# Feed-forward products with both parts of the activation in one 512-column matmul, and conditioning sums over rows of 1024

## The chip, the cores and the metric

The kernel runs on one core of a Trainium2 chip. A core has several engines that work side by side, each on its own queue of instructions: TensorE (in the profile PE for its matmuls and PEld for its weight loads), VectorE (DVE), ScalarE (ACT), GpSimd (POOL, nearly unused here), and SyncE (SP), which here issues the transfers. Work passes between engines by semaphores. Operands lie in SBUF; TensorE adds its results up in PSUM, which has eight banks of 512 float32 per partition.

The metric is the device time of one execution, in microseconds (us).

## The reference

The model is a trunk of two layers over 256 tokens of 1024 channels, in float32. Each layer is a feed-forward, a mixer (pooling in layer 0, differential attention in layer 1) and a second feed-forward, each under a norm whose scale, shift and gate come from a conditioning vector `c`:

```python
c_act = jax.nn.silu(c)
for i in range(DEPTH):                                   # 2
    mod = (c_act @ mod_w[i] + mod_b[i])[:, None, :]      # 1024 -> 9 * 1024
    sh0, sc0, g0, sh1, sc1, g1, sh2, sc2, g2 = jnp.split(mod, N_MOD, axis=-1)
    h = modulate(rms_norm(x, norm_g[i, 0]), sh0, sc0)
    x = x + 0.5 * g0 * swiglu(h, ffn_w_gu[i, 0], ffn_w_down[i, 0])
    h = modulate(rms_norm(x, norm_g[i, 1]), sh1, sc1)
    y = pool_mixer(h, ...) if i == 0 else diff_attention(h, ...)
    x = x + g1 * y
    h = modulate(rms_norm(x, norm_g[i, 2]), sh2, sc2)
    x = x + 0.5 * g2 * swiglu(h, ffn_w_gu[i, 1], ffn_w_down[i, 1])
return rms_norm(x, final_g)

def swiglu(h, w_gu, w_down):                             # 1024 -> 2 * 2816 -> 1024
    g, u = jnp.split(h @ w_gu, 2, axis=-1)
    return (jax.nn.silu(g) * u) @ w_down
```

There are four feed-forwards, of 34.6 MB of weights each, and 18 conditioning vectors of 1024, each from 4.2 MB of `mod_w`.

## The kernel before

**Split operands.** The products run in the type float32r, which keeps fewer bits than float32. So each operand is split into two parts, hi and lo, with hi + lo the float32 value. A product of two split operands is three matmuls, added up in PSUM: hi with hi, hi with lo, lo with hi. `prod3` (L341) issues them; its first operand is the one that TensorE loads (128 x 128), its second the moving one. In the feed-forward the weights are loaded and the activation moves: `hi` with `hh` (L343), `hi` with `hl` (L344), `lo` with `hh` (L345), each with a weight load of its own and 256 moving columns, the tokens. I call these three a triple.

**Weights.** `split_unit` (L278) fetches a unit of up to 512 rows by 256 columns (512 KB) into one of six `raw` buffers through SP's queue; ACT copies it to `hi` (L286) and DVE subtracts to `lo` (L287), seven buffers each. `unit` (L337) keeps five units prefetched.

**A feed-forward** (`ffn`, L490) has an up half of 11 steps. Step j makes two column blocks of 256, a gate block `pg` and an up block `pu`, each 16 triples over two units (`mm_half`, `mm_rows`, L451 and L460). The two 128-row results of a block lie side by side in one PSUM bank. ACT takes the SiLU of `pg` into SBUF (L511), DVE multiplies `pu` with it (L518), and the result is split into `ah`, `al` (L520). The down half has four blocks `dp` of 44 triples each over six units (`DOWN_K`); then `residual` (L405) adds the gated result to x and prepares the split operand `xh`, `xl` of the next stage, and `squares` (L412) adds up the sums that its norm needs.

In all but the first feed-forward the first two steps do not wait for the norm: `mm_deferred` (L435) multiplies the scaled x with two more columns for the shift (258 columns, L443 to L445), and the norm is applied to the result. In the first, five half blocks are begun early (`first_half`, L849), while the conditioning is worked out.

**Conditioning.** The first two vectors are worked out on TensorE at the start (`gemv_half`, L201). The 16 others are spread as steps between the blocks of the feed-forwards (`Background`, L260): six beside the first, four, five and one beside the others. A step of `gemv_steps` (L227) fetches two rows of 512 of `mod_w` per partition, 512 KB in all, and DVE adds them, times `cact`, to a sum of 512 columns (L239 the first, L241 the others): per vector 8 steps and 16 DVE instructions. At the end a matmul with ones (L246), a copy `row` (L249) and transposes (L252) turn two vectors at a time.

**PSUM.** `psum` hands out four single banks (tag `mm`), `psum2` two (tag `hd`), `psmall` two (tag `st`). The attention and the pooling mixer use the same functions.

**Order.** The program gives each instruction a priority by its place and by `high_priority`; a scheduler orders each engine's instructions at build time by these and by when buffers come free, so that PE's queue can interleave stages. On the chip every queue runs in that fixed order.

Of the kernel before, what the change touches and what calls it, by code (L numbers as in the profile page):

```python
# [33 lines left out]
U_BUFS = 8  # L34
# [3 lines left out]
def shape_constants():  # L38
    """Arrays that depend on the shapes alone: the pooling operator and the rotary tables."""
# [29 lines left out]
def trunk(ctx: ExitStack, tc: tile.TileContext, x, c, mod_w, mod_b, norm_g, w_gu, w_down, pool_w, pool_scale,  # L69
# [19 lines left out]

    def psum():  # L90
        return ps.tile([P, 512], F32, tag="mm", name=nm("mm"), bufs=4)

    def psum2():
        return ps.tile([P, 512], F32, tag="hd", name=nm("hd"), bufs=2)
# [21 lines left out]
    # ---------------------------------------------------------------- constants and small vectors  # L116
# [4 lines left out]
    # products on nothing, which bring the tensor engine to its full clock before the first data come  # L121
# [10 lines left out]
    hh = const([P, KD, T], "hh", F32R)  # L132
    hl = const([P, KD, T], "hl", F32R)
# [27 lines left out]
    # c and the rows of mod_w that it meets are dealt out eight in a row to a partition  # L161
# [8 lines left out]
    # ---------------------------------------------------------------- conditioning vectors  # L170
# [10 lines left out]
    def mod_done(i, p, k0=0, k1=KD):  # L181
        """Columns k0 to k1 of a conditioning vector are there: what the stages take from them."""
# [18 lines left out]
    def gemv_half(i, p, hf):  # L201
        """Half of silu(c) @ mod_w[i] + mod_b[i], 512 columns, transposed; on the tensor engine."""
        pt = psmall()
        # (while little else is there to do, products on nothing keep the tensor engine's clock up)
# [11 lines left out]
        row = t1k(512, "u", U_BUFS)  # L216
# [10 lines left out]
    def gemv_steps(parts):  # L227
        """The same for one or two parts, the sums over k tiles on the vector engine; a generator of steps."""
        n = 2 * len(parts)
        acc_ = [t1k(512, "u", U_BUFS) for _ in range(n)]  # L230
        for h in range(n):
            i, p = parts[h // 2]
            a = acc_[h]
            for q in range(4):
                rv = gemv_load(i, p, h % 2, q)
                for k in range(2):
                    kk = q * 2 + k
                    if kk == 0:
                        V.tensor_scalar(a, rv[:, k, :], cact[:, 0:1], None, ALU.mult)  # L239
                    else:  # L240
                        V.scalar_tensor_tensor(a, rv[:, k, :], cact[:, kk:kk + 1], a, ALU.mult, ALU.add)  # L241
                if h < n - 1 or q < 3:
                    yield
        pt = psmall()
        for h in range(n):
            PE.matmul(pt[h * 32:(h + 1) * 32, :], ones[:, 0:32], acc_[h], start=True, stop=True,  # L246
                      skip_group_check=True, tile_position=(0, h * 32))
        row = t1k(512, "u", U_BUFS)
# [11 lines left out]
    class Background:  # L260
        """Conditioning vectors worked out between the units of another stage, spread evenly over them."""
# [79 lines left out]
    def prod3(o, lh, ll, rh, rl, start, stop, **kw):  # L341
        """o += l^T r with both split."""
# [12 lines left out]
    # ---------------------------------------------------------------- norms  # L355
# [8 lines left out]
    def rsqrt_small(y, v, tiny=tiny):  # L364
        """y = v ** -0.5 on the vector engine: a first value from the exponent, then Newton steps."""
# [26 lines left out]
    def rstd_cols():  # L392
        """rstd of token q * 128 + p on partition p, column q."""
# [27 lines left out]
    def shift_cols(b):  # L421
        """The shift as two more columns of the moving operand."""
# [3 lines left out]
    def normalise(js, rstd, a, b):  # L426
        """h = x * a * rstd + b, split."""
# [7 lines left out]
    def mm_deferred(os_):  # L435
        """The products of one column block of 256 with x * a (and the shift); os_: the results of its two tiles."""
# [10 lines left out]
    def pair3(pt, m, lh, ll, rh, rl, first, last):  # L447
        """prod3 into half m of a bank whose halves are summed up side by side: the first product of half 0 clears it."""
        prod3(pt[:, m * T:(m + 1) * T], lh, ll, rh, rl, first and m == 0, last and m == 1, skip_group_check=True)

    def mm_half(pt, half, rh, rl, *ahead_):  # L451
        """Half of the products of one column block of 256 with 1024 rows of a split operand, transposed."""
# [10 lines left out]

    def shift_of(o):
# [4 lines left out]
    # ---------------------------------------------------------------- constants of the attention  # L469
# [19 lines left out]
    # ---------------------------------------------------------------- feed-forward  # L489
    def ffn(i, s, ndef, nxt, parts_up, parts_down, early=()):  # L490
        """nxt: scale of the next stage's norm, or None at the end."""
# [6 lines left out]
        for j in range(KF // 2):  # L498
# [4 lines left out]
            if j >= ndef:  # L503
                w = t1k(1024, "qk", 2)
                if early:
                    pg = early.pop(0)
                    mm_half(pg, 1, hh, hl)
                else:
                    pg = psum()
# [417 lines left out]
```

## Time and profile before

| | |
|---|---|
| median of 3 runs | 967.26 us (963.95 to 969.74) |
| span of the profiled execution, first to last instruction | 960.5 us |
| PE, PEld busy | 947.5, 911.9 us |
| DVE, ACT busy | 749.1, 498.6 us |
| HBM read | 234.34 MB, 245 GB/s over the span |
| transfers of `mod_w` | 144 of 512 KB, 5.7 us from issue to landing (median) |
| transfers of weights, up half | 176 of 512 KB, 5.2 us |

The page shows the profiled execution's span; the runs' times are a few microseconds longer, for what lies before the first and after the last instruction. Matmuls overlap in the array, so the duration of one (283 ns for 256 columns) is a latency; how often they start is what counts. A stretch of windows gives, for each engine, the busy time in it and the number of its instructions.

### The profile page before, as it was taken

What the parts mean: (1) busy time and instruction counts of PE and PEld (TensorE: products, weight loads), DVE (VectorE), ACT (ScalarE), POOL (GpSimd) and SP (SyncE); (2) the same over time, 40 slices, a digit from 0 to 9 for tenths busy, and PEclk for the clock granted to TensorE, in tenths of its full rate; (3) what the DMA queues carried; (4) which work ended last, traced back from release to release, by engine and by line L of the source; (5) the groups of instructions that cost most, each with busy time, mean ns of one, the idle gap of its engine ahead of it and who ended that gap; (6) DMA issues with size and microseconds to landing.
All of it is one profiled execution on the core that took longest, in us unless ns stands there. A gap on an engine that the chain in (4) does not pass through costs nothing.

```text
span 960.5 us, 19223 instructions
## 1 busy us (share of the span) xinstructions
PE 947.5 (99%) x7722; PEld 911.9 (95%) x7722; DVE 749.1 (78%) x1203; ACT 498.6 (52%) x759; POOL 0.7 (0%) x6
## 2 busy tenths in 40 slices
PE   8999999999999999999999999999999999999997
PEld 5699999999999999999999999989999999999996
DVE  3488889898998768888988788798888896664551
ACT  2354445455765445445654454367777764444541
POOL 0000000000000000000000000000000000000000
PEclk9999999999999999999999999999999999999999
DMA  8899999999469878997699888985544449765521
GB/s 280 285 337 319 325 319 321 317 346 292 140 192 344 268 242 277 312 313 255 195 344 315 289 280 300 297 286 168 153 135 128 140 154 292 234 222 180 181 78 44
DMA packets 201179, 237.69 MB, mean 247 GB/s; under 512 B 8113, under 2 KB 163074, under 8 KB 201090
## 3 DMA queue, kind: packets, MB, share of 16 engines
q1 hardware_dynamic: 200514, 235.42, 74.7%
q8 instruction: 60, 0.98, 0.4%
q10 hardware_dynamic: 576, 1.05, 0.3%
q14 instruction: 29, 0.24, 0.1%
HBM read 234.34 MB, written 1.05 MB: 245 GB/s over the span
## 4 chain that ended last, share of the span: by engine, by line
PE 91%; DVE 3%; DMA 3%; ACT 1%; issue 1%; SPq 0%; ACTq 0%; DVEq 0%
PE mm L343 22%; PE mm L344 21%; PE mm L345 21%; PE hd L344 4%; PE hd L345 4%; PE hd L343 4%; PE mm L445 2%; PE mm L443 2%; PE mm L444 2%; DMA raw<-in_mod_w_dram 1%; PE st L214 1%; PE st L246 1%; PE hd L655 1%; DVE lo L287 1%; DVE u L241 1%
## 5 line engine op out<-in xcount | busy, mean ns | idle before, releaser
L286 ACT ACTIVATE hi<-raw 128x1024 fp32r<-128x1024 f32 (+1 forms) x308 | 316.5, 1035 | 293.7 <-PE mm L344 146.1
L287 DVE TENSOR_TENSOR lo<-raw,hi 128x1024 fp32r<-128x1024 f32 (+1 forms) x308 | 363.5, 1192 | 57.7 <-ACT hi L286 54.5
L343 PE MATMUL mm<-hh,hi 128*128 128x256 f32 x992 | 280.2, 283 | 0.0
L345 PE MATMUL mm<-hh,lo 128*128 128x256 f32 x992 | 279.8, 283 | 0.0
L344 PE MATMUL mm<-hl,hi 128*128 128x256 f32 x992 | 279.7, 283 | 0.0
L343 PE MATMUL mm<-ahl,hi 128*128 128x256 f32 x768 | 217.4, 283 | 0.0
L344 PE MATMUL mm<-ahl,hi 128*128 128x256 f32 x768 | 216.6, 282 | 0.0
L345 PE MATMUL mm<-ahl,lo 128*128 128x256 f32 x768 | 216.1, 282 | 0.0
L241 DVE SCALAR_TENSOR_TENSOR u<-raw,cact,u 128x512 f32<-128x512 f32 x224 | 167.4, 749 | 55.4 <-DMA raw<-in_mod_w_dram 51.6
L343 PEld LDWEIGHTS mm<-hh,hi 128*128 128x128 f32 x992 | 186.8, 189 | 4.9 <-issue 3.4
L345 PEld LDWEIGHTS mm<-hh,lo 128*128 128x128 f32 x992 | 187.0, 189 | 1.1 <-issue 0.8
L344 PEld LDWEIGHTS mm<-hl,hi 128*128 128x128 f32 x992 | 186.9, 189 | 0.1
L343 PEld LDWEIGHTS mm<-ahl,hi 128*128 128x128 f32 x768 | 144.5, 188 | 6.2 <-issue 5.0
L344 PEld LDWEIGHTS mm<-ahl,hi 128*128 128x128 f32 x768 | 144.7, 188 | 0.9 <-issue 0.8
L345 PEld LDWEIGHTS mm<-ahl,lo 128*128 128x128 f32 x768 | 144.6, 188 | 0.0
L344 PE MATMUL hd<-hl,hi 128*128 128x256 f32 x288 | 81.4, 283 | 0.1
L343 PE MATMUL hd<-hh,hi 128*128 128x256 f32 x288 | 81.4, 283 | 0.0
L345 PE MATMUL hd<-hh,lo 128*128 128x256 f32 x288 | 81.2, 282 | 0.0
L444 PE MATMUL mm<-xl,hi 128*128 128x256 f32 x208 | 59.1, 286 | 0.0
L445 PE MATMUL mm<-xh,lo 128*128 128x258 f32 x208 | 58.6, 283 | 0.0
L443 PE MATMUL mm<-xh,hi 128*128 128x258 f32 x208 | 57.6, 283 | 0.1
L343 PEld LDWEIGHTS hd<-hh,hi 128*128 128x128 f32 x288 | 54.3, 189 | 1.8 <-ACT hh L432 0.9
(217 smaller groups left out, 1077.1 us busy)
## 6 DMA issues: line engine op xcount, KB each, us to landing
raw<-in_ffn_w_gu_dram SPq DMA_DIRECT2D x176, 512.0 KB, 5.2
raw<-in_mod_w_dram SPq DMA_DIRECT2D x144, 512.0 KB, 5.7
raw<-in_ffn_w_down_dram SPq DMA_DIRECT2D x64, 512.0 KB, 5.1
raw<-in_ffn_w_down_dram SPq DMA_DIRECT2D x32, 384.0 KB, 4.4
raw<-in_diff_w_qkv_dram SPq DMA_DIRECT2D x24, 512.0 KB, 4.8
raw<-in_diff_w_o_dram SPq DMA_DIRECT2D x8, 512.0 KB, 4.1
u<-in_x_dram ACTq DMA_DIRECT2D x4, 256.0 KB, 4.0
raw<-in_pool_w_dram SPq DMA_DIRECT2D x2, 512.0 KB, 6.1
```

Of the source, the lines that this page charges most:

```text
L214: PE.matmul(pt[r:r + 32, :], cwide[:, kk, :], rv[:, k, :], start=(kk < 4), stop=(kk >= 4), skip_group_check=True, tile_position=(0, r))
L241: V.scalar_tensor_tensor(a, rv[:, k, :], cact[:, kk:kk + 1], a, ALU.mult, ALU.add)
L246: PE.matmul(pt[h * 32:(h + 1) * 32, :], ones[:, 0:32], acc_[h], start=True, stop=True, skip_group_check=True, tile_position=(0, h * 32))
L286: S.activation(hi[:, :n], raw[:, :n], AF.Copy)
L287: V.tensor_tensor(lo[:, :n], raw[:, :n], hi[:, :n].bitcast(F32), ALU.subtract)
L343: PE.matmul(o, lh, rh, start=start, stop=False, **kw)
L344: PE.matmul(o, lh, rl, start=False, stop=False, **kw)
L345: PE.matmul(o, ll, rh, start=False, stop=stop, **kw)
L443: PE.matmul(o[:, :T + 2], hi[:, kk, cs], xh[:, k, :], start=(k == 0), stop=False)
L444: PE.matmul(o[:, :T], hi[:, kk, cs], xl[:, k, :], start=False, stop=False)
L445: PE.matmul(o[:, :T + 2], lo[:, kk, cs], xh[:, k, :], start=False, stop=(k == KD - 1))
L655: PE.matmul(sc[c2][:, q * T:(q + 1) * T], l[pr, 0, qs], r[pr, 1, :], start=(n == 0), stop=(n == 2))
```

## The change

**The wide product.** The two parts of the activation become one tile, `hhl`, with `hh` and `hl` as its halves (`ahl` was one already). `both` multiplies a hi tile with both at once, 512 moving columns, into a whole bank: hi with hh in the first half, hi with hl in the second. The lo tile meets `hh` alone, 256 columns, added to the second half. A block of two such banks is multiplied by `mm_wide` (up) or in the loop over `DOWN_K` (down). `fold` then copies the second halves to SBUF by ACT and adds the first ones by DVE; SiLU, product and residual read the result from SBUF. The early blocks, the deferred ones, the pooling mixer and the attention keep the triples.

**PSUM.** The banks are handed out in pairs: two of tag `mm`, one of tag `hd`. `wide` goes round over the three; `psum` and `psum2` hand out the halves of a pair one after the other.

**Conditioning.** A step fetches one row of 1024 columns per partition, again 512 KB, and adds it to a sum of 1024 columns: 8 DVE instructions per vector instead of 16. Four buffers of 1024 (tag `u`) take the place of eight of 512. Some users of that tag move to `qk`, among them `row`; others take a half of 1024.

Comments and docstrings are removed, so line numbers shift. The core of the diff:

```diff
-U_BUFS = 8
+U_BUFS = 4
...
+    def banks(tag, bufs):
+        return ps.tile([P, 2, 512], F32, tag=tag, name=nm(tag), bufs=bufs)
+    spare = {"mm": [], "hd": []}
+    def pair():
+        spare["mm"].clear()
+        return banks("mm", 2)
+    def pair2():
+        spare["hd"].clear()
+        return banks("hd", 1)
+    def one(tag, bufs):
+        if not spare[tag]:
+            t = banks(tag, bufs)
+            spare[tag] += [t[:, 0, :], t[:, 1, :]]
+        return spare[tag].pop(0)
     def psum():
-        return ps.tile([P, 512], F32, tag="mm", name=nm("mm"), bufs=4)
+        return one("mm", 2)
     def psum2():
-        return ps.tile([P, 512], F32, tag="hd", name=nm("hd"), bufs=2)
+        return one("hd", 1)
+    turn = [0]
+    def wide():
+        turn[0] += 1
+        return pair() if turn[0] % 3 else pair2()
...
-    hh = const([P, KD, T], "hh", F32R)
-    hl = const([P, KD, T], "hl", F32R)
+    hhl = const([P, 2, KD, T], "hhl", F32R)
+    hh, hl = hhl[:, 0], hhl[:, 1]
...
     def gemv_steps(parts):
         n = 2 * len(parts)
-        acc_ = [t1k(512, "u", U_BUFS) for _ in range(n)]
-        for h in range(n):
-            i, p = parts[h // 2]
-            a = acc_[h]
-            for q in range(4):
-                rv = gemv_load(i, p, h % 2, q)
-                for k in range(2):
-                    kk = q * 2 + k
-                    if kk == 0:
-                        V.tensor_scalar(a, rv[:, k, :], cact[:, 0:1], None, ALU.mult)
-                    else:
-                        V.scalar_tensor_tensor(a, rv[:, k, :], cact[:, kk:kk + 1], a, ALU.mult, ALU.add)
-                if h < n - 1 or q < 3:
+        acc_ = [t1k(1024, "u", U_BUFS) for _ in parts]
+        for e, (i, p) in enumerate(parts):
+            a = acc_[e]
+            for kk in range(KD):
+                raw = rawp.tile([P, 1024], F32, tag="raw", name=nm("raw"))
+                nc.sync.dma_start(raw, mod_w[i].rearrange("(p k) f -> p k f", p=P)[:, kk, p * D:(p + 1) * D])
+                if kk == 0:
+                    V.tensor_scalar(a, raw, cact[:, 0:1], None, ALU.mult)
+                else:
+                    V.scalar_tensor_tensor(a, raw, cact[:, kk:kk + 1], a, ALU.mult, ALU.add)
+                if e < len(parts) - 1 or kk < KD - 1:
                     yield
...
-        row = t1k(512, "u", U_BUFS)
+        row = t1k(512, "qk", 2)
...
+    def both(o, lh, ll, r, start, stop):
+        PE.matmul(o, lh, r, start=start, stop=False)
+        PE.matmul(o[:, T:], ll, r[:, 0, :], start=False, stop=stop)
+    def mm_wide(pt):
+        for half in range(2):
+            hi, lo = unit()
+            for m in range(2):
+                cs = slice(m * P, (m + 1) * P)
+                for kk in range(4):
+                    k = half * 4 + kk
+                    both(pt[:, m, :], hi[:, kk, cs], lo[:, kk, cs], hhl[:, :, k, :], k == 0, k == KD - 1)
+    def fold(out, pt):
+        S.activation(out, pt[..., T:], AF.Copy)
+        V.tensor_tensor(out, pt[..., :T], out, ALU.add)
...
                 else:
-                    pg = psum()
-                    mm_rows(pg, hh, hl)
-                S.activation(w[:, :512], pg, AF.Silu)
+                    pg = wide()
+                    mm_wide(pg)
+                    fold(w[:, :512].rearrange("p (m t) -> p m t", m=2), pg)
+                    S.activation(w[:, :512], w[:, :512], AF.Silu)
...
-                    pu = psum2() if j % 2 else psum()
-                    mm_rows(pu, hh, hl)
-                V.tensor_tensor(w[:, 512:], pu, w[:, :512], ALU.mult)
+                    pu = wide()
+                    mm_wide(pu)
+                    fold(w[:, 512:].rearrange("p (m t) -> p m t", m=2), pu)
+                    V.tensor_tensor(w[:, 512:], w[:, 512:], w[:, :512], ALU.mult)
...
-            po = psum()
+            po = wide()
...
-                            pair3(po, m, hi[:, k - k0, cs], lo[:, k - k0, cs], ah[:, k, :], al[:, k, :], k == 0, k == KF - 1)
+                            both(po[:, m, :], hi[:, k - k0, cs], lo[:, k - k0, cs], ahl[:, :, k, :], k == 0, k == KF - 1)
...
+                y = t1k(512, "qk", 2).rearrange("p (m t) -> p m t", m=2)
+                with tc.high_priority(offset=-100):
+                    fold(y[:, ms[0]:ms[-1] + 1, :], po[:, ms[0]:ms[-1] + 1, :])
                 if nxt or not last or ms[0] == 0:
-                    residual([js[m] for m in ms], [po[:, m * T:(m + 1) * T] for m in ms], g, a)
+                    residual([js[m] for m in ms], [y[:, m, :] for m in ms], g, a)
```

More of the change, by code (lines that the diff above doesn't have):

```diff
@@ L245, in gemv_steps @@
         for h in range(n):
-            PE.matmul(pt[h * 32:(h + 1) * 32, :], ones[:, 0:32], acc_[h], start=True, stop=True,
+            PE.matmul(pt[h * 32:(h + 1) * 32, :], ones[:, 0:32], acc_[h // 2][:, h % 2 * 512:(h % 2 + 1) * 512],
+                      start=True, stop=True,
                       skip_group_check=True, tile_position=(0, h * 32))
-        row = t1k(512, "u", U_BUFS)
+        row = t1k(512, "qk", 2)
         S.activation(row[:n * 32, :], pt[:n * 32, :], AF.Copy)
@@ L507, in ffn @@
                     mm_half(pg, 1, hh, hl)
+                    S.activation(w[:, :512], pg, AF.Silu)
                 else:
-                    pg = psum()
-                    mm_rows(pg, hh, hl)
-                S.activation(w[:, :512], pg, AF.Silu)
+                    pg = wide()
+                    mm_wide(pg)
+                    fold(w[:, :512].rearrange("p (m t) -> p m t", m=2), pg)
+                    S.activation(w[:, :512], w[:, :512], AF.Silu)
                 if early:
@@ L514, in ffn @@
                     mm_half(pu, 1, hh, hl)
+                    V.tensor_tensor(w[:, 512:], pu, w[:, :512], ALU.mult)
                 else:
-                    pu = psum2() if j % 2 else psum()
-                    mm_rows(pu, hh, hl)
-                V.tensor_tensor(w[:, 512:], pu, w[:, :512], ALU.mult)
+                    pu = wide()
+                    mm_wide(pu)
+                    fold(w[:, 512:].rearrange("p (m t) -> p m t", m=2), pu)
+                    V.tensor_tensor(w[:, 512:], w[:, 512:], w[:, :512], ALU.mult)
                 fs = slice(2 * j, 2 * j + 2)
@@ L522, in ffn @@
                 continue
-            pg = [psum(), psum()]
-            alloc = psum2 if j % 2 else psum
-            pu = [alloc(), alloc()]
+            pg, pu = wide(), wide()
+            pg, pu = ([t[:, m, :] for m in range(2)] for t in (pg, pu))
             sg = [t1k(), t1k()]
@@ L560, in ffn @@
                         for k in range(k0, k1):
-                            pair3(po, m, hi[:, k - k0, cs], lo[:, k - k0, cs], ah[:, k, :], al[:, k, :], k == 0, k == KF - 1)
+                            both(po[:, m, :], hi[:, k - k0, cs], lo[:, k - k0, cs], ahl[:, :, k, :], k == 0, k == KF - 1)
                     if ms[0] == 0:
                         back.tick()
+                y = t1k(512, "qk", 2).rearrange("p (m t) -> p m t", m=2)
+                with tc.high_priority(offset=-100):
+                    fold(y[:, ms[0]:ms[-1] + 1, :], po[:, ms[0]:ms[-1] + 1, :])
                 if nxt or not last or ms[0] == 0:
-                    residual([js[m] for m in ms], [po[:, m * T:(m + 1) * T] for m in ms], g, a)
+                    residual([js[m] for m in ms], [y[:, m, :] for m in ms], g, a)
                     squares([js[m] for m in ms])
                 else:
-                    residual([js[1]], [po[:, T:]], g)
+                    residual([js[1]], [y[:, 1, :]], g)
                     S.activation(sq7, xT[:, js[1], :], AF.Square)
@@ L601, in pool_mixer @@
             if g % 2:
-                cbt = t1k(512, *(("u", U_BUFS) if g < 2 else ("rope", 1)))
+                cbt = t1k(512, *(("qk", 2) if g < 2 else ("rope", 1)))
                 S.activation(cbt, pt, AF.Copy)
@@ L607, in pool_mixer @@
         for g in range(4):
-          z = t1k(512, "u", U_BUFS)
+          if g % 2 == 0:
+              zz = t1k(1024, "u", U_BUFS)
+          z = zz[:, g % 2 * 512:(g % 2 + 1) * 512]
           for q in range(NT):
@@ L660, in head_weights @@
             den = tinyw(4)
-            pe = [t1k(512, "u", U_BUFS) for _ in range(2)]
+            pe = t1k(1024, "u", U_BUFS)
+            pe = [pe[:, :512], pe[:, 512:]]
             for c2 in range(2):
@@ L818, in trunk @@
     for q in range(NT):
-        xq = [t1k(512, "u", U_BUFS) for _ in range(2)]
+        xq = t1k(1024, "u", U_BUFS)
+        xq = [xq[:, :512], xq[:, 512:]]
         for hf in range(2):
@@ L825, in trunk @@
         for hf in range(2):
-            S.activation(t1k(512, "u", U_BUFS), xin[q][hf], AF.Square, accum_out=ss[:, 2 * q + hf:2 * q + hf + 1])
+            S.activation(t1k(512, "qk", 2), xin[q][hf], AF.Square, accum_out=ss[:, 2 * q + hf:2 * q + hf + 1])
     v = tiny(NT)
@@ L897, in trunk @@
                 PE.transpose(pt[:, k * P:(k + 1) * P], xj[:, q * P:(q + 1) * P], ident)
-            ot = t1k(512, "u", U_BUFS)
+            if q == 0:
+                ott = t1k(1024, "u", U_BUFS)
+            ot = ott[:, q * 512:(q + 1) * 512]
             if q == 0:
```

## The prediction

> **What bounds the kernel now.** I began with the busy shares of the page.
>
> ```profile
> span 960.5 us, 19223 instructions
> ...
> PE 947.5 (99%) x7722; PEld 911.9 (95%) x7722; DVE 749.1 (78%) x1203; ACT 498.6 (52%) x759; POOL 0.7 (0%) x6
> ```
>
> TensorE and its weight loads are busy almost always, DVE four fifths. A busy PE need not be at its peak, so I read next, in the timeline, how far apart the products start.
>
> ```profile
> 300.00 0.28 PE L343 MATMUL mm<-hh,hi 128*128 128x256 f32 x1
> ...
> 302.97 0.28 PE L344 MATMUL mm<-hl,hi 128*128 128x256 f32 x1
> ...
> 800.04 0.29 PE L343 MATMUL hd<-hh,hi 128*128 128x256 f32 x1
> ...
> 803.04 0.28 PE L344 MATMUL hd<-hl,hi 128*128 128x256 f32 x1
> ...
> 258.56 0.28 PE L443 MATMUL mm<-xh,hi 128*128 128x258 f32 x1
> ...
> 261.68 0.28 PE L445 MATMUL mm<-xh,lo 128*128 128x258 f32 x1
> ...
> 15.06 0.59 PE L210 MATMUL mm<-raw,ident 128*128 128x256 f32 x2
> 15.28 0.59 PE L210 MATMUL mm<-raw,ident 128*128 128x256 f32 x2
> 15.49 0.38 PE L210 MATMUL mm<-raw,ident 128*128 128x256 f32 x1
> ```
>
> From 300.00 to 302.97 lie 25 starts: one product of 256 columns every 118.8 ns. From 800.04 to 803.04 another 25 come every 120.0 ns. From 258.56 to 261.68, where two in three have 258 columns, 26 come every 120.0 ns: the moving width does not separate these stretches. All three have one 128-column weight load per product. The products of L210 are plain fp32, which take longer over their 256 columns, and with the same weight load start every 215 ns (15.06, 15.28, 15.49): a load fits wholly behind a product that streams that long. I read 119 ns as the time of a weight load and its hand-over, with 256 columns streaming a little faster beneath it.
>
> Then the stages, by windows (columns: stretch, length, busy us of PE, PEld, DVE, ACT, POOL, granted clock, DMA share, GB/s).
>
> ```profile
> 53.00:172.00 119.00, 119.00 (x990) 116.07 (x989) 106.94 (x136) 57.09 (x68) 0.00 (x0) 1.00 0.98 325
> 175.00:237.00 62.00, 62.00 (x514) 60.05 (x513) 56.10 (x82) 31.67 (x43) 0.00 (x0) 1.00 1.00 327
> 258.00:282.00 24.00, 24.00 (x202) 23.91 (x201) 23.25 (x52) 17.08 (x27) 0.00 (x0) 1.00 0.69 215
> 282.00:377.00 95.00, 95.00 (x803) 94.27 (x801) 72.83 (x87) 43.48 (x52) 0.00 (x0) 1.00 0.82 270
> 379.00:442.00 63.00, 63.00 (x531) 61.98 (x530) 54.38 (x81) 29.35 (x39) 0.00 (x0) 1.00 0.94 316
> ...
> 472.00:570.00 98.00, 98.00 (x827) 97.03 (x826) 82.87 (x106) 47.53 (x56) 0.00 (x0) 1.00 0.91 301
> 573.00:637.00 64.00, 63.87 (x527) 61.73 (x526) 53.47 (x76) 28.66 (x38) 0.00 (x0) 1.00 0.91 303
> 642.00:748.00 106.00, 105.64 (x862) 101.03 (x862) 91.48 (x223) 78.42 (x193) 0.00 (x0) 1.00 0.48 146
> ...
> 788.00:878.00 90.00, 90.00 (x745) 88.82 (x744) 60.98 (x69) 41.99 (x49) 0.00 (x0) 1.00 0.74 237
> 878.00:943.00 65.00, 65.00 (x549) 65.00 (x549) 29.69 (x36) 27.72 (x37) 0.00 (x0) 1.00 0.36 118
> ```
>
> These are, in order, the up and down halves of the four feed-forwards, with the first deferred column blocks (258) and the attention (642) between. The clock is full. PE never idles, but the first feed-forward has DMA at 0.98 to 1.00 and DVE at 90%: there two others are nearly as late as PE.
>
> **The change, part by part.** *The wide product.* Three products with three loads (hi with hh, hi with hl, lo with hh) become two with two. How many:
>
> ```profile
> L343 PE MATMUL mm<-hh,hi 128*128 128x256 f32 x992 | 280.2, 283 | 0.0
> ...
> L343 PE MATMUL mm<-ahl,hi 128*128 128x256 f32 x768 | 217.4, 283 | 0.0
> ...
> L343 PE MATMUL hd<-hh,hi 128*128 128x256 f32 x288 | 81.4, 283 | 0.0
> ```
>
> Of 992 + 288 triples, 64 are the attention's q and k and 80 the five early blocks; of the 768, 64 are the attention's output product. That leaves 1136 + 704 = 1840 changed triples. A triple now costs 3 x 118.8 = 356 ns. After: the lo load hides behind the 512 columns, as a load does behind L210, so 215 ns for the wide product, then 119 for the narrow one, beneath which the next hi is loaded: 334 ns. The wide price is not in this trace. Its lower end is the 215 of L210 (under twice a 256-column stream it cannot go, and 256 columns stream in at most 119), its upper end two of today's products, 238. In between lies 119 + 107 = 226, if the 11 ns over L210's rate (215 / 2) belong to each instruction and not to its load. I take 215, the row whose stream and load lie nearest. Gross: 1840 x 22 ns = 40.5 us; by 226 it is 20 us, by 238 nothing.
>
> [...]
>
> *The fold.* Each changed block gets one ACT copy and one DVE addition out of PSUM. Prices:
>
> ```profile
> L287 DVE TENSOR_TENSOR lo<-raw,hi 128x1024 fp32r<-128x1024 f32 x276 | 333.5, 1220 | 46.7 <-ACT hi L286 43.5 <-DMA pk<-qk 1.6
> L241 DVE SCALAR_TENSOR_TENSOR u<-raw,cact,u 128x512 f32<-128x512 f32 x224 | 167.4, 749 | 55.4 <-DMA raw<-in_mod_w_dram 51.6
> ...
> L408 DVE SCALAR_TENSOR_TENSOR xT<-mm,G,xT 128x256 f32<-128x256 f32 x44 | 19.6, 478 | 19.0 <-PE mm L345 19.0
> ...
> L239 DVE TENSOR_SCALAR u<-raw,cact 128x512 f32<-128x512 f32 x32 | 15.4, 482 | 12.1 <-DMA raw<-in_mod_w_dram 12.1
> L518 DVE TENSOR_TENSOR qk<-mm,qk 128x512 f32<-128x512 f32 x21 | 14.4, 687 | 4.5 <-PE mm L345 4.3
> ...
> L249 ACT ACTIVATE u<-st 128x512 f32<-128x512 f32 x7 | 4.1, 589 | 5.8 <-PE st L246 5.8
> ```
>
> Up: 18 blocks in three feed-forwards, 17 in the first; down: 4 each: 87 folds. Addition like L518, 0.69 us; copy like L249, 0.59 us. DVE +60 us, ACT +51 us (52% to about 58%). The SiLU and the product stay, now from SBUF, at about the same price.
>
> *Conditioning in rows of 1024.* STT goes from 478 ns (256, L408) to 749 (512, L241): 271 per 256 elements, so 1024 cost about 1.29 us; the first, by L239 and the bounds 482 and 964, I take at 0.75. A vector goes from 2 x 0.482 + 14 x 0.749 = 11.45 us to 0.75 + 7 x 1.29 = 9.8: 1.7 saved, 16 vectors, 27 us of DVE. The DMAs stay 8 per vector of 512 KB, in the same places on SP's queue; rows are twice as long. [...]
>
> *Stage by stage* (PE after; DVE after = window + folds - 1.7 per vector; DMA as before):
> up 1: PE 119 - 17 x 16 x 0.022 = 113.0; DVE 106.9 + 11.7 - 6.8 = 111.8; DMA 0.98 x 119 = 116.6.
> down 1: PE 62 - 176 x 0.022 = 58.1; DVE 55.4; DMA 62.
> up 2: 88.7; 81.8; 78. down 2: 59.1; 53.7; 59.2.
> up 3: 91.7; 90.2; 89. down 3: 60.1; 52.8; 58.2.
> up 4: 83.7; 71.7; 67. down 4: 61.1; 32.4; 23.
> So the first feed-forward meets the DMA. What was prefetched (six raw, seven split buffers) covers part of it: I let it lose 4.9 of its 9.9 us, and the other near ties 1.5 together.
>
> *The ends of stages.* The next stage's products need the residual of the last block, which now waits for the fold, 0.59 + 0.69 = 1.28 us. Is there cover?
>
> ```profile
> 442.37 0.88 DVE L408 SCALAR_TENSOR_TENSOR xT<-mm,G,xT 128x256 f32<-128x256 f32 x2 [0.80 <-PE mm L345]
> ...
> 445.83 0.67 PE L383 MATMUL st<-acc,ones 128*128 128x256 f32 x2 [0.17 <-DVE acc L419]
> ```
>
> DVE waits for PE at once, and 3.5 us later PE already waits for the sum over squares: no cover left. Three joints at 1.28 plus the tail, where half a fold (0.8) stands bare: 4.6 us.
>
> *PSUM in pairs of banks.* Eight banks stay. Where single banks are handed out two at a time (pool, attention), a pair comes free only when both halves are read; A2 then waits for A0 and B0's residual behind one unit of PE work. Below: nothing, PE has scores to do; above: an eviction (0.6) plus queue at each of about ten pairs, 10 us. I take 2. The wide blocks rotate over three pairs, so a fold has two blocks, 10.7 us, of time. The deferred stretch at 258, where DVE has 23.25 of 24 us, starts with a thinner prefetch: 2 us.
>
> Sum: 40.5 - 4.9 - 1.5 - 4.6 - 2 - 2 = 25.5. The profiled span is 960.5, so 935.0. The runs' median, 967.26, is 6.8 us over the span, which I take as what lies around it: **942 us** (941.8).
>
> **The rivals.**
>
> *Fixed cost per product* (226 for the wide one): gross 20; the first feed-forward now fits the DMA better (loses 1), joints, pairs and prefetch as before less 1: 7.6. About 955. For it: no fp32r product of 512 columns is in the trace. Against: 258 columns cost no more than 256.
>
> ```profile
> SPq L284 <- DVE lo L287: 280.6, 178, 8.3
> ```
>
> *DMA and DVE take more*: feed-forward 1 gains nothing (-9.9), down 2, up 3 and down 3 half (-7), joints and pairs 6.6, deferred stretches 5: 12 net, 955. For it: the DMA share of 1.00; the row above, by which the transfers' queue waited 281 us for raw buffers that DVE's splits free, so a later DVE makes later transfers.
>
> *Slower: the wait in DVE's queue.* Each fold's addition stands behind the copy, and the copy behind the last product; behind the addition stand the splits of the next weights and the conditioning sums. Today's pattern for a wait on PE:
>
> ```profile
> DVE qk L518 <- PE hd L345: 6.4, 7, 1.5
> DVE qk L518 <- PE mm L345: 4.3, 6, 1.1
> ```
>
> 10.7 us over 38 is 0.28 each, which the slack of 1 to 7 us per stage just takes. If each new addition idles DVE for copy plus hand-over, 0.9 us, DVE sets up 1 at 127.1, up 2 at 98.0, up 3 at 106.4, up 4 at 87.9: 419.4 against today's 402, 17.4 more, while the downs keep 12.7 (3 x 3.9 and 1 in the first) and joints, pairs and deferred stretches cost 8.6: 13.3 slower, 981. It turns slower from about 0.7 us per fold. Against: the order can place other work between copy and addition. [...]
>
> *It doesn't do what it says*: what holds a product at 119 ns stays with every 256 columns, so a wide one costs 238; gross nothing, joints, pairs and deferred stretches stay: 8.6 slower, 976. For it: no row separates load from stream at 256 columns. Against: L210's 215. [...]
>
> **How the numbers follow.** Forecast 942 (own range 932 to 950): 0.55. Fixed cost: 0.14. DMA and DVE: 0.15. DVE's queue: 0.10. Wide costs two: 0.06. The low end is 929, nearly all of the 40.5 kept; up to 961 takes in the first three cases and leaves out about 2 in 10. Half a per cent, 4.8 us, is about what a measurement tells from no change. Faster than 962.4: 0.55 + 0.14 + 0.12 = 0.81. Within: 0.08, from the edges of the last three. Slower: 0.11.
>
> **What would show it.** Starts in a steady stretch alternating 215 and 119 ns (226 or 238 for the rivals); weight loads 5882 in number (7722 - 1840); down 4 near 61 us and up 4 near 84, which have no DMA or DVE limit; up 1 at about 116 with DMA near 1.0; DVE's sums at 1.29 us; about 1.3 us more PE idle at each joint. I am wrong if up 4 does not shorten, if PE idles several us inside up 1 or up 3 for lo tiles, or if the attention grows by over 5 us.

## The result, and the profile after

The changed kernel takes **990.61 us** (median of 4 runs, 989.39 to 991.71); the kernel before, run beside it, 965.61 us. The ratio is 1.0263, with a 95% interval of 1.0225 to 1.0301: **slower by 2.6%**, where 942 us was forecast. From the page:

```profile
span 987.4 us, 15579 instructions
...
PE 950.8 (96%) x5882; PEld 827.4 (84%) x5882; DVE 781.9 (79%) x1163; ACT 541.0 (55%) x847; POOL 0.7 (0%) x6
...
L491 PE MATMUL mm<-hhl,hi 128*128 128x512 f32 x768 | 271.3, 394 | 0.0
...
L265 DVE SCALAR_TENSOR_TENSOR u<-raw,cact,u 128x1024 f32<-128x1024 f32 x112 | 143.6, 1282 | 51.0 <-DMA raw<-in_mod_w_dram 50.2
```

The weight loads fell to 5882, as forecast, and a conditioning sum of 1024 columns takes 1.28 us (forecast 1.29). But 1840 fewer products did not lower PE's busy time (947.5 before), and PE now idles 37 us of the span, where it idled 13. The profiled execution took 989.39 us, 2.0 more than its span, so 2 us lie around a span, not the 6.8 that I added: the profiled execution of before was one of the quicker ones.

Where the 26.9 us of span came from, by the start of the first and last product of each stage in the two traces (the last column is `e_best`, the best version found below):

| stretch, us | before | after | best |
|---|---|---|---|
| start, to the first feed-forward product | 29.9 | 35.3 | 29.7 |
| up 1, up 2, up 3, up 4 together | 451.7 | 444.8 | 446.5 |
| down 1, down 3, down 4 together | 196.4 | 193.8 | 190.4 |
| down 2 | 64.9 | 70.3 | 65.8 |
| pooling, to the first deferred product | 14.9 | 21.2 | 21.5 |
| deferred blocks of feed-forward 2 | 24.9 | 28.2 | 24.9 |
| deferred blocks of feed-forwards 3 and 4, first products of the attention's heads | 72.2 | 71.5 | 72.9 |
| attention | 96.6 | 111.6 | 96.5 |
| after the last product | 9.0 | 10.7 | 9.9 |

The ups gained 6.9 us of a gross 25 forecast for them (1136 triples of 22 ns), and three of the downs 2.6. The start, down 2, the pooling, the deferred blocks behind it, the attention and the end lost 37 together. The windows of after (columns as in the prediction) show how:

```profile
171.00:236.00 65.00, 65.00 (x368) 55.01 (x367) 57.63 (x69) 33.31 (x45) 0.00 (x0) 1.00 0.92 309
236.00:257.00 21.00, 15.22 (x104) 12.89 (x102) 17.98 (x37) 13.22 (x22) 0.00 (x0) 0.92 0.85 276
257.00:285.00 28.00, 27.19 (x224) 26.94 (x224) 26.90 (x59) 19.97 (x35) 0.00 (x0) 1.00 0.41 124
...
387.00:457.00 70.00, 66.32 (x376) 56.38 (x368) 56.63 (x71) 34.26 (x47) 0.00 (x0) 0.98 0.88 283
...
676.00:789.00 113.00, 102.31 (x801) 96.38 (x802) 88.06 (x205) 75.90 (x192) 0.00 (x0) 0.92 0.41 127
811.00:914.00 103.00, 103.00 (x586) 89.20 (x586) 78.45 (x96) 58.09 (x78) 0.00 (x0) 1.00 0.73 230
```

and of before, for the pooling and the attention:

```profile
234.00:248.00 14.00, 13.48 (x112) 13.07 (x111) 12.92 (x33) 9.84 (x20) 0.00 (x0) 1.00 0.58 180
...
662.00:759.00 97.00, 96.64 (x788) 92.19 (x788) 83.40 (x199) 73.64 (x187) 0.00 (x0) 1.00 0.46 143
```

Inside the ups PE never idles (busy 118.00, 100.00, 104.00 and 103.00 us of windows of 118, 100, 104 and 103; 811 to 914 is the last of them), so no engine took over there; the products themselves are hardly faster. In the attention PE was 96.64 of 97 us busy; now it idles 10.7 us and its granted clock falls to 0.92. What PE waits for is in the view of waits (us in total, times, longest), of after:

```profile
PE st L785 <- ACT o L778: 5.4, 2, 4.6
PE st L277 <- ACT qk L274: 5.0, 3, 3.1
PE mm L368 <- ACT hhl L457: 2.6, 1, 2.6
PE hd L368 <- ACT ahl L374: 2.5, 1, 2.5
```

Before, no wait of PE on another engine came to more than 1.1 us in total. So there are three questions: the price of the wide product, the waits in attention and start, and L274, which is the copy `row` of the conditioning, now in tag `qk`. A fourth, the longer pooling, is taken up last.

### The profile page after: what moved, and what is told of

It is laid out like the page before. It is cut to its first block, busy times and chain, and to the rows that moved or that the text cites. A ratio compares the mean times of both kernels' runs of the same rounds, so it can differ in the third digit from the quotient of the medians.

```text
span 987.4 us, 15579 instructions
## 1 busy us (share of the span) xinstructions
PE 950.8 (96%) x5882; PEld 827.4 (84%) x5882; DVE 781.9 (79%) x1163; ACT 541.0 (55%) x847; POOL 0.7 (0%) x6
## 3 DMA queue, kind: packets, MB, share of 16 engines
q10 hardware_dynamic: 576, 1.05, 0.3%
HBM read 234.34 MB, written 1.05 MB: 238 GB/s over the span
## 4 chain that ended last, share of the span: by engine, by line
PE 73%; DMA 11%; DVE 9%; ACT 3%; issue 3%; ACTq 0%; SPq 0%; DVEq 0%
PE mm L491 21%; PE hd L491 12%; PE mm L492 11%; DMA raw<-in_mod_w_dram 8%; PE hd L492 6%; DVE lo L312 3%; PE mm L368 3%; PE mm L369 3%; PE mm L370 3%; PE mm L468 2%; PE mm L469 2%; PE mm L470 2%; PE st L240 1%; DVE u L265 1%; PE mm L236 1%
## 5 line engine op out<-in xcount | busy, mean ns | idle before, releaser
L491 PE MATMUL mm<-hhl,hi 128*128 128x512 f32 x768 | 271.3, 394 | 0.0
L492 PE MATMUL mm<-hhl,lo 128*128 128x256 f32 x768 | 217.2, 283 | 0.0
L265 DVE SCALAR_TENSOR_TENSOR u<-raw,cact,u 128x1024 f32<-128x1024 f32 x112 | 143.6, 1282 | 51.0 <-DMA raw<-in_mod_w_dram 50.2
L491 PEld LDWEIGHTS mm<-hhl,hi 128*128 128x128 f32 x768 | 144.2, 188 | 35.3 <-ACT qk L558 0.8
L491 PE MATMUL mm<-ahl,hi 128*128 128x512 f32 x440 | 156.7, 397 | 0.0
L492 PEld LDWEIGHTS mm<-hhl,lo 128*128 128x128 f32 x768 | 144.4, 188 | 0.3
L491 PE MATMUL hd<-hhl,hi 128*128 128x512 f32 x368 | 130.6, 394 | 0.0
L492 PE MATMUL hd<-hhl,lo 128*128 128x256 f32 x368 | 104.4, 284 | 0.0
L491 PEld LDWEIGHTS mm<-ahl,hi 128*128 128x128 f32 x440 | 83.3, 189 | 22.3 <-issue 1.7
L491 PE MATMUL hd<-ahl,hi 128*128 128x512 f32 x264 | 93.6, 395 | 0.3 <-DVE qk L507 0.3
```

The lines of the kernel that those rows point to most:

```text
L265: V.scalar_tensor_tensor(a, raw, cact[:, kk:kk + 1], a, ALU.mult, ALU.add)
L491: PE.matmul(o, lh, r, start=start, stop=False)
L492: PE.matmul(o[:, T:], ll, r[:, 0, :], start=False, stop=stop)
```

## The experiments

Times are medians; ratios are to the kernel before, run beside each. For short: "pairs" are the banks handed out in pairs, "row" is the move of the conditioning's copies from tag `u` to `qk`.

**The price of a product.** Two kernels (one execution each) issue matmuls, 64 of a kind, on operands that lie in SBUF already: 256, 384 and 512 columns, 512 in two stretches, 256 with 32 columns loaded, and the changed kernel's pair, of which these lines are the first and the last:

```diff
+    for n in range(N):
+        PE.matmul(a256[:, :256], wt[:, n % 8, :], lin[:, n % 4, :256], **ends(n))
...
+    for n in range(N):
+        PE.matmul(mix, wt[:, n % 8, :], mov[:, :, n % 4, :], start=(n == 0), stop=False)
+        PE.matmul(mix[:, 256:], wt[:, (n + 3) % 8, :], mov[:, 0, n % 4, :], start=False, stop=(n == N - 1))
```

> A kernel that only measures: rows of 64 float32r products each, every one with its own weight load; nothing of the reference is computed. Theory 'load': 119 ns between products of 256 columns is the time of a 128-column weight load, so 384 columns would start every 161 to 165 ns, 512 every 215, and 256 columns with a load of only 32 columns every 108 to 110. Theory 'stream': each column costs about 0.45 ns whatever is loaded, so 384 come to 172 to 176, 512 to 226 to 238, and 256 with the short load stay at 117 to 120. Theory 'two runs': only a moving operand in two stretches of 256 is slow, so 512 contiguous columns come to 215 and 512 in two stretches to 231.

By line: least, median and longest duration in ns, first and last start in us.

```profile
L47 PE MATMUL a<-lin,wt x64: 283/283/284, 20.7 to 28.3; 128*128 128x256 f32 x64
...
L50 PE MATMUL a<-lin,wt x64: 334/334/339, 28.4 to 39.3; 128*128 128x384 f32 x64
...
L53 PE MATMUL a<-lin,wt x64: 387/389/397, 39.5 to 53.8; 128*128 128x512 f32 x64
...
L59 PE MATMUL few<-lin,wt x64: 280/280/281, 68.5 to 76.0; 128*32 128x256 f32 x64
...
L62 PE MATMUL mix<-mov,wt x64: 395/398/404, 76.1 to 98.3; 128*128 128x512 f32 x64
```

First to last start over 63 (the starts are read to 0.1 us, 1.6 ns of the mean): 120 ns for 256 columns, 173 for 384, 227 for 512, whether in one stretch or two. 32 loaded columns instead of 128, whose load is 108 ns instead of 192, still give 118: at 256 columns the time of the weight load does not set the pace. The three fit 0.418 ns per column and 13 ns per product. Every product here has a load of its own, so whether the 13 ns belong to the product or to its having a load at all is not shown. And the alternating pair, which is what the changed kernel issues, costs 353 ns, 6 more than 227 + 120. The second kernel asks where the 6 ns come from:

> A kernel that only measures, as m_price: alternating products of 512 and 256 columns, 64 of each, the narrow one added to the second half of the wide one's bank (as in the changed kernel), to the first half, and to a bank of its own; and three of 256 in the order of a triple. If the 6 ns that a pair costs above 227 + 120 = 347 come from two products meeting in the same columns of a bank: 353 in the first row, 347 in the others. If they come from the change of width: 353 in all three. Three of 256 columns: 360 in either case.

With the narrow product on the same half, on the other half, or in a bank of its own the pair costs 353 each time, and three products of 256 columns 360: the 6 ns come with the change of width, not with the columns that are added to. The timeline of the changed kernel shows the same cadence:

```profile
300.17 0.28 PE L492 MATMUL mm<-hhl,lo 128*128 128x256 f32 x1
300.29 0.39 PE L491 MATMUL mm<-hhl,hi 128*128 128x512 f32 x1
300.52 0.28 PE L492 MATMUL mm<-hhl,lo 128*128 128x256 f32 x1
...
302.98 0.28 PE L492 MATMUL mm<-hhl,lo 128*128 128x256 f32 x1
```

120 ns after the narrow product, 230 after the wide one; 8 triples in 2.81 us, 351 each against 356 before. A triple gains 3 ns (353 against the 356 of before), 5 (351 against 356) or 7 (353 against 360), by which rows one compares: 6 to 12 us over 1840, not 40.5.

**The parts of the change, undone or alone.** `e_single` is the changed kernel with single banks, so that a fold is two copies and two additions. `e_pairs` is the kernel before with banks in pairs; a block of triples takes a pair and leaves its second bank empty. `e_cond` is the kernel before with the new conditioning, row moved. The diffs are cut to their core:

```diff
 # e_single, against after
+        return ps.tile([P, 512], F32, tag="mm", name=nm("mm"), bufs=4)
-        return pair() if turn[0] % 3 else pair2()
+        f = psum if turn[0] % 3 else psum2
+        return [f(), f()]
 # e_pairs, against before
-        return ps.tile([P, 512], F32, tag="mm", name=nm("mm"), bufs=4)
+        return one("mm", 2)
-            po = psum()
+            po = wide()[:, 0, :]
 # e_cond, against before: gemv_steps and the tags of after
-        row = t1k(512, "u", U_BUFS)
+        row = t1k(512, "qk", 2)
```

> The changed kernel with single PSUM banks (four and two) as before; a wide block takes two of them and its fold is two copies and two additions of 256 columns. Theory 'pairs' (banks that come free two at a time cost the start, the pooling, the attention and the joints some 27 us): 955 to 966, the attention back from 112 to about 97 us, the pooling from 21 to about 15. Theory 'queue' (the fold's waits in the queues of ACT and DVE are the loss): 988 to 996, since there are more fold instructions than before.

> The kernel before, with the banks handed out in pairs and nothing else of the change: three products per triple, no fold. Theory 'pairs': 985 to 995, with the start, pooling and attention longer as in the changed kernel. Theory 'queue': 964 to 972.

> The kernel before, with the conditioning over rows of 1024 and its buffers, row copy and scratch in the other tag, and nothing else of the change. Theory 'pairs': 960 to 968, within half a per cent of before or a little faster, DVE some 24 us less busy. A theory that the moved row buffer (its transposes held TensorE for 3 us at one place) carries the loss: 972 to 980.

Measured: `e_single` 969.24, ratio 1.0043 (1.0021 to 1.0064); `e_pairs` 989.65, 1.0255 (1.0211 to 1.0299); `e_cond` 977.82, 1.0127 (1.0078 to 1.0176). The pairs alone cost 24 us, with start (36.5) and attention (113.6) as long as in the changed kernel. The conditioning alone costs 12.6, as the theory of the moved row had it. `e_single` missed both of its ranges: the pairs are not the whole loss, and PE waits 8.0 us on the row there too. In `e_cond`'s view of waits and in its timeline:

```profile
PE st L251 <- ACT qk L248: 11.3, 4, 5.2
```

```profile
375.94 1.07 PE L244 MATMUL st<-u,ones 128*32 128x512 f32 x8
...
379.32 1.29 DVE L239 SCALAR_TENSOR_TENSOR u<-raw,cact,u 128x1024 f32<-128x1024 f32 x1 [2.08 <-DMA raw<-in_mod_w_dram]
380.53 0.69 DVE L517 TENSOR_TENSOR qk<-mm,qk 128x512 f32<-128x512 f32 x1
...
381.25 0.63 ACT L348 ACTIVATE ahl<-qk 128x512 fp32r<-128x512 f32 x1 [4.21 <-DVE qk L517]
...
381.78 0.58 ACT L248 ACTIVATE qk<-st 128x512 f32<-128x512 f32 x1
...
382.42 1.11 PE L251 MATMUL st<-ident,qk 128*128 128x128 f32 x4 [4.04 <-ACT qk L248]
```

The sums of PE are done at 377, but the copy `row` shares two `qk` buffers with the feed-forward's blocks. In ACT's queue it now stands behind the split of the block before it, which waits 4.2 us for DVE, and DVE had stood for 2.1 us before a conditioning transfer. PE's transposes (L251) stand in front of the next products: PE waits 4 us. In tag `u` the copy shared no buffer with these blocks.

So the row was put back, alone, with everything but the pairs, and in the changed kernel; and the wide product was run alone:

```diff
 # e_cond_row against e_cond; e_best against e_single; e_row against after
-        row = t1k(512, "qk", 2)
+        row = t1k(512, "u", U_BUFS)
 # e_wide, against e_single: gemv_steps, U_BUFS and the tags of before
-        acc_ = [t1k(1024, "u", U_BUFS) for _ in parts]
+        acc_ = [t1k(512, "u", U_BUFS) for _ in range(n)]
```

> The conditioning over rows of 1024 alone, as in the run e_cond, with the row copy back in the tag u. Theory 'row' (the copy gets its buffer only behind the split of a feed-forward tile, and TensorE's transposes wait for it 11.3 us in all): 961 to 968, the wait of TensorE on the row copy under 2 us. Theory 'DVE's longer sums block the weights' splits': 973 to 980, that wait unchanged or replaced by waits for lo tiles.

> The wide product and the fold alone: single banks, conditioning, buffers and row copy as before. Theory 'parts add up' (pairs +24, conditioning +13, wide product -8): 954 to 960. Theory 'the fold's waits eat what the wide product saves': 963 to 970.

> All of the change except the pairs of banks and the moved row copy. If parts add up: 951 to 959, faster than both kernels. If the row copy is not the cause of the conditioning's loss: 966 to 971, as e_single.

> The changed kernel whole, banks in pairs, with the copy row of the background conditioning alone back in tag u. Theory 'row's wait for a qk buffer costs wherever it is': it cost 16.8 us in the kernel with old banks and triples; the changed kernel shows waits of 5 us on it (PE st L277 from ACT qk L274), so here it gives back 3 to 16 us: 975 to 987, the most of it in down 2. Rival 'it costs nothing in the changed kernel, since the pairs' waits hide it': 989 to 992.

| kernel | us | ratio (95%) |
|---|---|---|
| `e_cond_row`: before + rows of 1024 | 961.06 | 0.9949 (0.9932 to 0.9966) |
| `e_wide`: before + wide product and fold | 966.88 | 1.0024 (1.0003 to 1.0046) |
| `e_best`: before + both | **959.39** | 0.9931 (0.9908 to 0.9953) |
| `e_row`: after, row in `u` | 980.85 | 1.0162 (1.0131 to 1.0194) |

The row costs 16.8 us in the kernel of before (977.82 to 961.06), 9.8 with the wide product (969.24 to 959.39) and 9.8 in the changed kernel (990.61 to 980.85). The pairs cost 24 alone, 21.4 to 21.5 in the others (980.85 against 959.39, 990.61 against 969.24). In `e_cond_row` PE's wait on the row is gone from the view of waits, and in the changed kernel 5.5 of the 9.8 us come back in down 2 (70.3 to 64.7). Without both, `e_best` beats both kernels, just above its expected 951 to 959. Its 6.9 us come mostly from the conditioning: the wide product alone gains nothing, against my expectation that the parts would add up. In `e_wide` the pooling takes 22.9 us (14.9 before), and PE waits 3.3 us in up 3 for a conditioning sum, late on DVE; that is as much as its products gain.

**Where the pairs cost.** Three edits of the changed kernel, of two executions each: the attention's four output blocks (A0 to A3) get pairs of their own, or only one of the tags goes back to single banks (there a wide block takes two of them).

```diff
 # e_attn
+                if n == "A" and u % 2 == 0:
+                    own = banks("mm", 2)
-                    os_.append(psum())
+                    os_.append(own[:, u % 2, :])
 # e_hd
-        return one("hd", 1)
+        return ps.tile([P, 512], F32, tag="hd", name=nm("hd"), bufs=2)
 # e_mm
-        return one("mm", 2)
+        return ps.tile([P, 512], F32, tag="mm", name=nm("mm"), bufs=4)
```

> The changed kernel, with the attention's four output blocks in two pairs of banks of their own (A0 with A1, A2 with A3). Theory 'A2 and A3 have no bank until B0 is done, and B0 waits for the last heads': the attention goes from 112 to 103 to 107 us, TensorE's wait of 4.6 us on the last normalised heads shrinks below 2, the total comes to 981 to 986. If the pairs cost the attention by other ways: 988 to 992.

> The changed kernel with tag hd as two single banks again and tag mm still in pairs. If the attention's loss lies in its scores, whose two banks now come free together (hd): attention from 112 to 96 to 101 us, start and pooling unchanged, total 974 to 980. If it lies in the projections (mm): attention within 2 us of 112, total 986 to 992.

> The changed kernel with tag mm as four single banks again and tag hd still a pair. If the projections' banks (mm) carry the attention's loss: attention 96 to 101 us, and the start 4 to 5 us shorter as well, total 968 to 976. If the scores' banks (hd) carry it: attention above 106, only the start shorter, total 983 to 988.

`e_attn` took 988.44 (attention 108.8, the wait on `o` 2.6 instead of 4.6 us), `e_hd` 988.10 (112.3), both no great help: the intervals of their ratios (1.0189 to 1.0279 and 1.0190 to 1.0282) overlap that of the changed kernel. `e_mm` took 980.44: its attention is 95.9 and its start 30.3, as before. So the pairs of tag `mm` carry both losses. It missed its expected total, since its waits on the row grew to 12.1 us (5.0 in the changed kernel) and its pooling to 27.0; why that grew is open. It is also 11 us above `e_single`, which has no pairs at all, 5.0 of them in down 2 (75.4 against 70.4) and 3.7 in the pooling (27.0 against 23.3). So the pair of `hd` is not free there, though by itself it carries neither start nor attention.

At the start the mechanism is plain. Before (in the row of a window, the third number from the end is the granted clock):

```profile
0.00:20.00 20.00, 16.40 (x79) 11.67 (x80) 4.09 (x20) 5.94 (x13) 0.70 (x6) 1.00 0.80 283
...
10.03 1.99 PE L210 MATMUL mm<-raw,ident 128*128 128x256 f32 x8 [0.57 <-ACT xT L840]
...
19.01 0.60 ACT L217 ACTIVATE u<-st 128x512 f32<-128x512 f32 x1 [8.54 <-PE st L214]
```

After:

```profile
0.00:20.00 20.00, 15.18 (x60) 10.43 (x61) 4.10 (x20) 5.41 (x12) 0.71 (x6) 0.83 0.67 231
...
12.97 1.22 PE L236 MATMUL mm<-raw,ident 128*128 128x256 f32 x2 [1.71 <-DVE xT L895]
...
23.60 0.60 ACT L243 ACTIVATE qk<-st 128x512 f32<-128x512 f32 x1 [10.73 <-PE st L240]
```

The idle products (L210 before, L236 after; nothing reads their results) got a bank at 10.0; as half of a pair it comes free only when both transposes of x in it are copied out, at 13.0 (a wait of 1.71 us). They stand ahead of the conditioning in PE's queue, and its first half ends at 23.6 instead of 19.0. The granted clock was lower meanwhile: 0.83 over the first 20 us, where it was 1.00. In the attention the trace of after shows the end of the chain:

```profile
765.79 1.28 ACT L778 ACTIVATE o<-o,tinyv 128x128 f32<-128x128 f32 x4 [2.40 <-DVE tinyv L387]
766.25 1.35 PE L785 MATMUL st<-ident,o 128*128 128x128 f32 x4 [4.60 <-ACT o L778]
```

and its window with the granted clock, and behind them an earlier wait of the same attention with the window that follows it:

```profile
756.00:772.00 16.00, 10.28 (x61) 8.78 (x60) 7.66 (x24) 7.04 (x23) 0.00 (x0) 0.76 0.21 66
...
689.28 0.58 PE L368 MATMUL mm<-hi,hhl 128*128 128x256 f32 x1 [2.59 <-ACT hhl L457]
...
692.00:708.00 16.00, 16.00 (x123) 15.05 (x122) 11.66 (x20) 8.74 (x19) 0.00 (x0) 0.87 0.35 108
```

`e_mm`, for comparison, over its attention:

```profile
676.00:783.00 107.00, 103.07 (x864) 97.88 (x863) 91.88 (x222) 80.16 (x200) 0.00 (x0) 1.00 0.45 141
```

At 761.6 PE has nothing left but what waits for the last head's norm; before, other products covered it, and PE was idle for 0.4 us of the whole attention. After the waits the clock is lower: 0.76 in the 16 us that hold the wait of 4.6 us, and 0.87 in the 16 us from 692 on, in which PE was never idle, behind the wait of 2.6 us (to 689.28) and one of 0.67 (to 690.96). The lower clock is a second loss: from 693.26 to 695.82, inside a stretch at 0.50 (692 to 696), products of 256 columns start every 213 ns, where the kernel before starts them every 119. Over the attention's 113 us the clock is 0.92; in `e_mm`, where these waits are gone, it is 1.00. How the pairs of `mm` push the other products out of the way, beyond the part that `e_attn` took back, is not shown.

**The pooling.** It is 6.6 us longer in `e_best` too, which has neither pairs nor the moved row. With the new conditioning alone it is not (14.8 in `e_cond_row`), with the wide product and fold alone it is (22.9 in `e_wide`). Here z is the normalised result that the mixer's next products need. Two attempts: the last block's fold, residual and squares ahead in the queues (`e_joint`), and the norm chain with z ahead of the weight splits (`e_rstd`).

```diff
 # e_joint, against e_best
-                with tc.high_priority(offset=-100):
+                with tc.high_priority(offset=500 if end else -100):
                     fold(y
 # e_rstd, against e_best
+        with tc.high_priority(offset=500):
+            rstd = rstd_cols()
...
+          with tc.high_priority(offset=500):
+            for q in range(NT):
```

> As e_best, with the fold, residual and squares of the last block of each feed-forward's down half put ahead in the queues of ACT and DVE. Theory 'queue at the joints' (the residual waits behind splits and conditioning sums, and the pooling starts 7 us late): pooling from 21.5 to 15 to 17.5 us, total 951 to 956. If the pooling is late for another reason: 957 to 962.

> The kernel with single banks, wide products, rows of 1024 and the copy row in its old tag, with one edit: the pooling's norm chain (three small DVE instructions and one of ACT) and its z stand ahead of the weight splits in the queues. Only one split of 1.22 us is left between the chain's first and last instruction, where that kernel has three and before has two. Theory 'splits within the norm chain and behind it make the pooling late': the pooling stretch falls from 21.5 to 17 to 19 us, the time from 959.4 to 955 to 958. Rival 'the loss moves: the splits put off are then late for the deferred blocks or the second feed-forward': the pooling stretch falls, the deferred stretch or up 2 grows by as much, and the time stays at 958 to 961. Rival 'z is late because the sums over squares are late, not because of what stands in the chain': the pooling stretch stays at 20 to 21.5 us.

`e_joint` took 964.99, ratio 1.0000 (0.9980 to 1.0020), pooling 21.4: the last residual starts at 231.2 instead of 231.7, and the pooling is no shorter, so the fold's place in the queues is not what makes it late. The total is above both expected ranges, 5.6 us more than `e_best`; its trace is of its quickest execution, 959.73, and does not show where they go. `e_rstd` took 961.24, ratio 0.9955 (0.9935 to 0.9975), pooling 21.8. Its chain did get shorter; in DVE's timeline of `e_best`:

```profile
237.27 0.16 DVE L404 TENSOR_SCALAR tiny<-st 128x2 f32<-128x2 f32 x1
...
241.35 0.15 DVE L368 SCALAR_TENSOR_TENSOR rstdc<-tiny,tiny 128x2 f32<-128x2 f32 x1
```

and of `e_rstd`, DVE first, then ACT and PE:

```profile
237.01 0.16 DVE L404 TENSOR_SCALAR tiny<-st 128x2 f32<-128x2 f32 x1 [2.00 <-PE st L402]
...
238.60 0.16 DVE L368 SCALAR_TENSOR_TENSOR rstdc<-tiny,tiny 128x2 f32<-128x2 f32 x1
```

```profile
238.80 3.16 ACT L292 ACTIVATE hi<-raw 128x1024 fp32r<-128x1024 f32 x3
241.97 2.19 ACT L355 ACTIVATE ahl<-u 128x512 fp32r<-128x512 f32 x4
```

```profile
243.70 0.39 PE L349 MATMUL hd<-hi,ahl 128*128 128x256 f32 x1 [2.88 <-ACT ahl L355]
```

The norm is there 2.75 us earlier, but three `hi` copies of prefetched weights stand ahead of the split of z on ACT, and PE waits as long as before (2.9 against 3.2 us). So the expectation failed, and so did its reason as put. What is seen is that weight splits, 1.05 us each on ACT and 1.2 on DVE, fall in front of the mixer's short chain: six `hi` copies between the last down product (230.0) and the first split of z (243.5) in `e_best`, two before (233.6 to 241.5). Why more of them fall there was not settled.

## Why the prediction was wrong

**The wide product: "I take 215".** This step failed, and it is the largest. I read 119 ns as the time of a weight load because 256 and 258 columns cost the same, and L210 as proof that a load hides behind 215 ns of stream. The rows are as quoted, but they don't separate load from stream: 2 columns are 0.8 ns by the fit of `m_price`. With the load cut to 32 columns the product still takes 118 there. And L210 is another kind of product. In the view of lines of before:

```profile
L210 PE MATMUL mm<-raw,ident 128*128 128x256 f32 x32 | 8.8, 402 | 0.6 <-ACT xT L840 0.6
```

The program issues 16 of these plain fp32 products (two in each of four rounds, for two vectors), and the trace has 32 records: each of the starts 215 ns apart is half of one. So the row was no stand-in for 512 columns of float32r. The bound 226, by a fixed cost per instruction, is what a run of wide products measures (227); in the alternation a wide product holds the next one off for 230 ns in the changed kernel and 240 to 250 in the first pairs of `m_price` (76.08 to 77.39), on either side of my upper bound of 238. Gross 6 to 12 us instead of 40.5.

**PSUM in pairs: "I take 2", bounds 0 to 10.** Second failure, by size and by place: 21 to 24 us. I priced evictions of single blocks and held that PE would have other work meanwhile. In the start (+5.4) and the attention (+15.0) it had none, and the granted clock was lower as well (0.83 over the first 20 us, 0.92 over the attention). I also thought only of the attention and pooling, not of the idle products at the start. That the attention would wait with A2 behind A0 and B0 was a small part: `e_attn` took away 2.8 of the 15.

**A move costed at nothing, by silence.** The front tells that `row` goes to tag `qk`; the prediction didn't price it. It costs 9.8 us.

**Joints, 4.6.** The fold's prices were right (copy 0.58, addition 0.69 us measured), and the tail's 0.8 is what `e_best` shows (9.0 to 9.9). At the joints to deferred blocks no loss is seen in `e_best`; at the pooling 6.6 us are, and `e_joint` shows that the fold's place in the queues is not their cause.

**Prefetch, 2.** With pairs the deferred blocks lose 3.3, without them nothing: and `e_pairs`, with the old prefetch and triples, loses 3.4 (28.3): it was the pairs.

**Feed-forward 1 against the DMA, 4.9, and near ties, 1.5.** Never tested, since the products didn't get fast enough: up 1 gained 1.2, down 1 2.0.

**Conditioning.** Sizes right; alone it gains 5 us where I gave it no gain of its own.

**The rivals.** The slower rivals named DVE's queue and a wide product at the price of two. PE never waits on a fold inside the ups of the changed kernel, so the first is out; the second had the price nearly right, but it had 8.6 us of side costs where the pairs and the row alone cost 31. Of the three signs by which I said I would be wrong, one came outright, the attention's 15 us, and one in part: up 4 did shorten, but by 2.6 us where 288 triples of 22 ns are 6.3. The third, PE idle inside up 1 or up 3, did not come.

## What to carry to other kernels

To know whether a matmul is held by its load or its stream, measure a row that changes one of them; two rows that change both, or neither by enough, or that are of another type, carry nothing, and forty microseconds hung on them. When buffers are regrouped or moved to another tag, list every user of both tags and ask, for each, what stands behind it in its engine's queue and what PE has left to do: here one small copy in a shared tag cost 9.8 us and pairs of banks 21, together more than the 25.5 us forecast for the whole change. Idle time of TensorE cost twice in the attention here, at waits of 2.6 and 4.6 us: once as a wait and once as the clock behind it, with products every 213 ns instead of 119 where it was 0.50.

## What the runs showed of the hardware

A float32r product takes 120, 173 and 227 ns from start to start for 256, 384 and 512 columns, with a weight load of 128 columns for each, which 0.418 ns per column and 13 ns per product fit; at 256 columns a load of 32 gives 118 (`m_price`). Alternating 512 and 256 columns costs about 6 ns per pair more (353 against 347), wherever the results are added (`m_mix`). In the changed kernel waits of TensorE of 2.6 and 0.7 us were followed by a granted clock of 0.87 over 16 us, and one of 4.6 us lay in 16 us at 0.76; at a granted clock of 0.50 products of 256 columns started every 213 ns, at 1.00 every 119.
